# An encoder of dilated and neighbourhood attention on one core: bias loads spread, one gate through ScalarE, splits and per-head norms moved to GpSimd, bias lines as fp32r matmuls

## The chip, the cores and the metric

The kernel runs on one core of a Trainium2 chip. Times are device microseconds of one execution of the whole program; a program is timed by the median of several runs. The engines are TensorE (PE in the profile, its weight loads PEld), VectorE (DVE), ScalarE (ACT), GpSimd (POOL) and SyncE (SP), which here issues most of the DMA transfers. Each engine takes its instructions in the order in which they stand in its own stream, and waits on semaphores for what other engines deliver. PSUM is the memory that matmuls write to, in banks; SBUF holds everything else on chip.

## The reference

One batch of 512 tokens, width 1024, 16 heads of 64, two layers, everything in float32. Layer A is dilated sliding-window attention with three dilation groups, layer B neighbourhood attention on an 8 x 64 grid. Each layer normalises its input, projects it, norms q and k per head, attends with a bias, multiplies by a SiLU gate, projects back and adds the residual. Cut to its core:

```python
def rms_norm(x, g):
    y = x * lax.rsqrt(jnp.mean(x * x, axis=-1, keepdims=True) + RMS_EPS)
    return y * g

def mixer_a(hn, w_in, w_out, q_gain, k_gain, t5_bias):
    proj = hn @ w_in                       # q, k, v of 3 groups x 16 heads, and the gate
    for g, (window, dilation) in enumerate(((128, 1), (512, 4), (2048, 16))):
        q = rms_norm(qkv[:, :, g, 0], q_gain[g])      # per head, over 64 values
        k = rms_norm(qkv[:, :, g, 1], k_gain[g])
        o, lse = dilated_group_attention(q, k, qkv[:, :, g, 2], t5_bias[g], dilation, reach)
    alpha = softmax(stack(lses), axis=0)
    return (sum(alpha * stack(outs)) * silu(gate)) @ w_out

def reference(x, ...):
    x = x + mixer_a(rms_norm(x, norm_gain[0]), ...)
    x = x + mixer_b(rms_norm(x, norm_gain[1]), ...)   # 2-D window, relative bias, same gate
    return x
```

## The kernel before

**Float32 from three matmuls.** TensorE's fp32r format is less exact than float32, so each operand is split: a high part rounded to fp32r (`h`) and a low part, the value less its high part (`l`). A product is then three fp32r matmuls, high by high, high by low and low by high (`mm3`). Weights are split on the way: a raw tile of 128 x 1024 (`wraw`, eight slots) is loaded by a DMA; ACT casts 512 columns of it to the high part (`wh`, six buffers, function `cast`, line 160), then POOL or DVE subtracts to make the low part (`wl`, five buffers, `rest`, line 167). Such a half tile is called a job here and numbered in the order in which TensorE uses it; there are 344. `splits` (line 298) runs ahead of TensorE by the depth of these buffers, and `pool[0]` (line 302) says which jobs' subtraction goes to POOL: none of the first sixteen jobs behind those of the first projection, then every second in the rest of layer A's input projections, then two in five.

**Layer A** works on head pairs `hc` = 0 to 7. For each pair there are q and k of the three groups, v, and the gate. From pair 1 on, the q and k projections are done with fewer products by sums of quarter matrices ("mixed" jobs; `b11`, `t2` and the like in `Plan.mixed` are raw tiles of it): some weight tiles are added up on the way, by POOL's own accumulating DMAs (`Plan.add`) and by DVE. While TensorE projects pair `hc + 1`, the attention of pair `hc` goes on beside it.

**The order.** TensorE's order is made by hand: `run` (line 1173) interleaves a main generator (the projections) with a side generator (the attention), on a clock that counts the estimated time of the matmuls issued so far. A generator yields times to wait by that clock; `later_on(delay, job)` (line 350) issues a piece of work when the clock has gone on by `delay` nanoseconds. The other engines' instructions are given through `Ordered.call` (line 86, so nearly everything but matmuls bears line 86 in the profile) and stand, once `held[0]` is set (from pair 0's k projection on), in the order in which the program gives them.

**The per-head norms.** The sum of squares of each head, `ss`, is an ACT square and a DVE reduction (`squares`). `head_norm` (line 439) then makes `rs`, the inverse root, by `rsqrt` (line 139): two DVE operations for a first guess (`nv` is the mean with epsilon) and three Newton steps of three operations, eleven in all on a 128 x 32 tile (q) or 128 x 16 (k), since there are eight or four heads for each of four token blocks. Four scalings by `rs` follow on DVE (`rawq` or `rawk`), and DVE takes its turn of weight subtractions between them. Their gains are folded in `gk` (line 505), which ACT applies to k.

**The biases.** `bias_lines` (line 578) makes layer A's bias once: three matmuls in plain float32 of a bucket table (`t5`, 32 x 48) with a one-hot matrix (`oh`, 32 x 896) into the bank `pl`; DVE subtracts that from a mask (`mk`), and SP writes the lines to DRAM (`l0_d`, `l12_d`). For each pair `bias_a` (line 894) loads the six tiles that its attention subtracts from its logits (`log`): two of 128 x 256 into `e0` and four of 128 x 224 into `e12`, each partition with its own shift of a line. For pairs from 2 on the call (line 1145) stands after the projection of v of the pair before; SP then issues all six one after the other. SP also issues the weight tiles, the class reordering of v (`pt`) and the store of each pair's result (`y_d`).

**The gates.** In layer B, `main_g` (line 1305) projects a pair's gate into a PSUM bank `acc`; DVE multiplies it by the row scale into `gt`, which frees the bank, and ACT takes the tanh. The three minima, exponentials (`p`, with `mn` the row's minimum and sum) and transposes of the attention (`tr`) share DVE and ACT with it.

Of the kernel before, what the change touches and what calls it, by code (L numbers as in the profile page):

```python
# [49 lines left out]
def tile_hybrid_encoder(  # L50
# [14 lines left out]
    cp = ctx.enter_context(tc.tile_pool(name="cp", bufs=1))  # L65
    big = ctx.enter_context(tc.tile_pool(name="big", bufs=1))
    wp = ctx.enter_context(tc.tile_pool(name="wp", bufs=3))
    wk = ctx.enter_context(tc.tile_pool(name="wk", bufs=2))
# [4 lines left out]
    held = [False]  # L73
# [24 lines left out]
    vec, act, pol, syn = (Ordered(e) for e in (nc.vector, nc.scalar, nc.gpsimd, nc.sync))  # L98
# [21 lines left out]
    make_identity(nc, ident)  # L120
    ones = wp.tile([P, S], F32R, tag="wh", name="ones", bufs=6)
    vec.memset(ones.bitcast(F32), 1.0)
    one = cp.tile([P, 1], F32, name="one")
    vec.memset(one, 1.0)

    xm_d = dr.tile([P, KT, S], F32, name="xm_d")
# [9 lines left out]
    mix_h = big.tile([P, 4, 4, H], F32R, tag="yh", name="mix_h")  # L136
    mix_l = big.tile([P, 4, 4, H], F32R, tag="yl", name="mix_l")

    def rsqrt(eng, r, ss, n, scale):
        v = wk.tile([P, 32], F32, tag="nv", name="nv", bufs=1)  # L140
        a = wk.tile([P, 32], F32, tag="na", name="na")
        eng.tensor_scalar(v[:, :n], ss, scale, EPS, op0=ALU.mult, op1=ALU.add)
        eng.tensor_scalar(
            r.bitcast(I32), v[:, :n].bitcast(I32), -0.5, float(0x5F3759DF), op0=ALU.mult, op1=ALU.add
        )
        for _ in range(3):
            eng.tensor_mul(a[:, :n], r, r)
            if eng is vec:
                eng.scalar_tensor_tensor(a[:, :n], a[:, :n], -0.5, v[:, :n], op0=ALU.mult, op1=ALU.mult)
                eng.scalar_tensor_tensor(r, a[:, :n], 1.5, r, op0=ALU.add, op1=ALU.mult)  # L150
                continue
            eng.tensor_mul(a[:, :n], a[:, :n], v[:, :n])
            eng.tensor_scalar(a[:, :n], a[:, :n], -0.5, 1.5, op0=ALU.mult, op1=ALU.add)
            eng.tensor_mul(r, r, a[:, :n])

    turn, pool = [0], [[2, 5]]
# [103 lines left out]
    mixed_jobs = len(plan.jobs)  # L260
# [24 lines left out]
    def load(raw):  # L285
        home(raw)
        if raw.off is None:
            return
        dst, src = raw.tile[:, : raw.cols], w[:, raw.off : raw.off + raw.cols]
        if not begun:  # L290
            syn.dma_start(dst[:, :512], src[:, :512])
            begun.append(load_x(1, 2))
            dst, src = dst[:, 512:], src[:, 512:]
        syn.dma_start(dst, src)
        if behind:
            behind.pop()()

    def splits():
        casts, queue, due = [], [], plan.loads(lead)
        for at, (raw, c, step, n) in enumerate(plan.jobs):  # L300
            first = at - start_jobs
            pool[0] = [0, 1] if first < 16 else [1, 2] if at < mixed_jobs else [2, 5]
            for r in due.get(at, ()):
                load(r)
            for add in plan.sums.get(at, ()):
                add()
            casts.append((cast(raw.tile[:, c : c + step], step), n))
            if len(casts) > 1:
                done, m = casts.pop(0)
                queue.append((*rest(*done), m))  # L310
            if len(queue) > 4:
                yield queue.pop(0)
        done, m = casts.pop(0)
        queue.append((*rest(*done), m))
        yield from queue
# [10 lines left out]
    def matmul(o, l, r, share=1, **kw):  # L326

        cols = max(r.free_size() / 2.4, l.free_size() / 1.2)
        clock[0] += (cols if r.dtype == F32R else r.free_size() * 4 / 2.4 * l.free_size() / P) / share
        nc.tensor.matmul(o, l, r, **kw)  # L330
# [19 lines left out]
    def later_on(delay, job):  # L350

        timers.append((clock[0] + delay, job))
        timers.sort(key=lambda t: t[0])
# [82 lines left out]
    def squares_soon(*args):  # L436
        later_on(800, partial(squares, *args)) if held[0] else squares(*args)

    def head_norm(raw, ss, ns):


        rs = wk.tile([P, 32], F32, tag="rs", name="rs")
        rsqrt(vec, rs[:, : 4 * ns], ss[:, : 4 * ns], 4 * ns, 1.0 / DH)

        def scale(i):
            by = rs[:, i * ns : (i + 1) * ns].unsqueeze(2).to_broadcast([P, ns, 64])
            v = raw[:, i, : ns * 64].rearrange("p (a b) -> p a b", b=64)
            return vec.tensor_mul(v, v, by)

        for i in range(4):  # L450
            later_on(600 + 1000 * i, partial(scale, i)) if held[0] else scale(i)
# [52 lines left out]
    hg = xn[:, 2 * KT : G]  # L504
    gk = cp.tile([P, 4], F32, name="gk")
    for i, (a, b) in enumerate(((0, 3), (1, 4), (2, 5), (6, 7))):
        vec.scalar_tensor_tensor(
            gk[:, i : i + 1], hg[:, a : a + 1], -SCALE, hg[:, b : b + 1], op0=ALU.mult, op1=ALU.mult
        )

    def norm(layer, k, xk):
# [66 lines left out]
    def bias_lines():  # L578

        oh = wk.tile([32, 896], F32, tag="k12", name="oh", bufs=1)  # L580
        tc.keep_in_program_order(syn.dma_start(oh, onehot))
        t5 = wk.tile([32, 48], F32, tag="e0", name="t5", bufs=1)
        syn.dma_start(t5, t5t)
        mk = wk.tile([16, 896], F32, tag="q12", name="mk", bufs=1)
        syn.dma_start(mk, maskc)
        yield 3000
        for g, (o, n) in enumerate(((0, 384), (384, 256), (640, 256))):
            pl = bank("pl")
            matmul(pl[0:16, :n], t5[:, 16 * g : 16 * g + 16], oh[:, o : o + n], start=True, stop=True)
            vec.tensor_sub(mk[:, o : o + n], mk[:, o : o + n], pl[0:16, :n])  # L590
        for j in range(4):
            syn.dma_start(l0_d[:, j, j : j + 384], mk[:, 0:384])
        syn.dma_start(l12_d, mk[:, 384:896])
        yield
# [16 lines left out]
    st = {}  # L611
# [39 lines left out]
    def normed(raw, ss, ns, key, hc):  # L651

        def go():
            with in_order() if hc == 0 else nullcontext():
                head_norm(raw, ss, ns)
            st[key, hc] = raw
            stamp[key, hc] = clock[0]

        if (key, hc) == ("rawk", 0):
            later_on(4000, go)  # L660
        elif held[0]:
            later_on(2200, go)
        else:
            go()
# [226 lines left out]
            pol.tensor_sub(l, src, h.bitcast(F32))  # L891
        stamp["ya", hc, "y"] = 0

    def bias_a(hc):
        e0 = wk.tile([P, 2, 256], F32, tag="e0", name="e0", bufs=1)
        e12 = wk.tile([P, 4, 224], F32, tag="e12", name="e12", bufs=1)
        for hd in range(2):
            h = 2 * hc + hd
            syn.dma_start(
                e0[:, hd, :],  # L900
                bass.AP(l0_d.tensor, l0_d.offset + h * 1600 + 127, [[400, 4], [-4, 32], [1, 256]]),
            )
            for g in range(2):
                syn.dma_start(
                    e12[:, 2 * hd + g, :],
                    bass.AP(l12_d.tensor, l12_d.offset + h * 512 + 256 * g + 31, [[0, 4], [-1, 32], [1, 224]]),
                )
        return e0, e12

    def bias_b(hc):  # L910
# [47 lines left out]
    def attn_a(hc):  # L958
        e0, e12 = st.pop(("e", hc))
# [182 lines left out]
        yield from v_a(hc)  # L1142
        yield "wait", ("pt", hc), 2500 if hc else 0
        if hc:
            st["e", hc + 1] = bias_a(hc + 1)
        if hc:
            yield "wait", ("border", hc + 1), 0
        yield "wait", ("gate", hc), 4000
# [120 lines left out]
    def main_qk(n):  # L1269

        raw, ss = part(n), sums()

        def evac(i, acc):
            act.activation(raw[:, i, :], acc, AF.Copy, scale=rs_n[:, i : i + 1])
            squares(raw[:, i, :], ss, i, 8)

        guard = ("qk", 2 * n - 3) if n else ("rs", "b")
        yield from project(tile_of(hn_h), tile_of(hn_l), 512, evac, guard)
        rs = wk.tile([P, 32], F32, tag="rs", name="rs")
        rsqrt(vec, rs, ss, 32, 1.0 / DH)  # L1280

        def scale(hc):
            h = 4 * (hc % 2)
            by = rs.rearrange("p (i h) -> p i h", i=4)[:, :, h : h + 4].unsqueeze(3).to_broadcast([P, 4, 4, 64])
            v = raw[:, :, 64 * h : 64 * h + 256]
            u = v.rearrange("p i (h c) -> p i h c", c=64)
            vec.tensor_mul(u, u, by)
            return v

        for hc in (2 * n, 2 * n + 1):  # L1290
            st["raw", hc] = partial(scale, hc)
            stamp["raw", hc] = clock[0]
# [12 lines left out]
    def main_g(hc):  # L1305
        acc = []
        yield from project_t(acc)
        yield ("yb", hc - 3, "y") if hc else ("rs", "all")
        third = dict(tag="e0", bufs=1) if hc % 3 == 2 else dict(tag="gt", bufs=2)
        gt = wk.tile([P, S], F32, name="gt", **third)  # L1310
        eg = wk.tile([P, S], F32, tag="eg", name="eg", bufs=1)
        tc.keep_in_program_order(vec.tensor_mul(gt, acc[0], st["rs_half"]))
        act.activation(eg, gt, AF.Tanh)
        gated(hc, gt, eg, "gate_b")

# [286 lines left out]
```

## Time and profile before

| | us |
|---|---|
| median of 3 runs | 836.58 |
| the runs | 836.58, 831.44, 837.23 |
| the profiled execution | 832.24 |
| its span on the core (first to last instruction) | 830.4 |
| TensorE busy | 817.5 |
| VectorE busy | 619.4 |
| ScalarE busy | 511.5 |
| GpSimd busy | 271.9 |

Between the span and the profiled execution's own time lie 1.84 us of start and end. TensorE's mean granted clock in it is 0.998 of full speed. The page has this slicing of the span into 40 stretches of 20.8 us; a digit is the busy share in tenths:

```profile
PE   9999999999999999999999999999999999999998
DVE  7898896897897797787786777647656758686553
ACT  8666756855855846846855837654567476766340
POOL 0073343453452542543542515321111221122220
```

Layer A fills the first two thirds, layer B the rest. How to read on: TensorE is the engine to look at, so the stretches in which it stands still are what a change can win; a busy share of another engine, averaged over the span, says little about the few places where TensorE waits for it.

### The profile page before, as it was taken

The page shows a single profiled execution, that of the slowest core. Times are in us where ns is not written, and L with a number is a line of the kernel's source. Part 1 is how long each engine was busy: PE and PEld are TensorE (multiplying, and loading weights), DVE is VectorE, ACT ScalarE, POOL GpSimd, SP SyncE. Part 2 cuts the span into 40 slices and gives each one's busy share as a digit, 9 for nine tenths or more (in the row PEclk, how much of TensorE's full clock was granted, in tenths as well). Part 3 has the DMA queues.
Part 4 walks back from the last instruction along what each step waited for, and adds up shares of the span by engine and source line. Part 5 has one row for each costly group of instructions (what it writes and reads, how often), then busy time and mean ns, then how long its engine had stood idle before and what let it go on. Part 6 is the DMA issues. An engine that isn't in the chain of part 4 may idle for free.

```text
span 830.4 us, 17546 instructions
## 1 busy us (share of the span) xinstructions
PE 817.5 (98%) x6418; PEld 660.8 (80%) x6418; DVE 619.4 (75%) x1568; ACT 511.5 (62%) x1056; POOL 271.9 (33%) x214
## 2 busy tenths in 40 slices
PE   9999999999999999999999999999999999999998
PEld 7877878888887887888887887788888787788776
DVE  7898896897897797787786777647656758686553
ACT  8666756855855846846855837654567476766340
POOL 0073343453452542543542515321111221122220
PEclk9999999999999999999999999999999999999999
DMA  9327665676676766785775664284255574635122
GB/s 349 141 62 187 173 162 142 123 174 209 118 185 205 163 162 183 161 184 168 160 158 182 146 183 166 92 309 142 93 164 134 156 205 132 192 100 151 36 102 101
DMA packets 54725, 131.92 MB, mean 159 GB/s; under 512 B 6768, under 2 KB 24112, under 8 KB 54512
## 3 DMA queue, kind: packets, MB, share of 16 engines
q1 hardware_dynamic: 48304, 108.40, 42.0%
q0 software_dynamic: 6048, 22.02, 15.1%
q8 instruction: 50, 0.82, 0.4%
q10 hardware_dynamic: 288, 0.39, 0.2%
q14 instruction: 35, 0.29, 0.1%
HBM read 111.73 MB, written 11.72 MB: 149 GB/s over the span
## 4 chain that ended last, share of the span: by engine, by line
PE 81%; DVE 7%; ACT 4%; DMA 4%; issue 2%; ACTq 0%; SPq 0%; DVEq 0%
PE acc L330 68%; PE log L330 5%; PE o L330 5%; PE tp L334 3%; DMA wraw<-in_w 3%; DVE wl L86 2%; ACT p L86 1%; ACT wh L86 1%; DMA yr<-y_d 1%; DVE rawq L86 1%; DVE na L86 1%; DVE p L86 1%; DVE ss L86 1%; DVE rs L86 1%; DVE rawk L86 0%
## 5 line engine op out<-in xcount | busy, mean ns | idle before, releaser
L86 POOL TENSOR_TENSOR wl<-wraw,wh 128x512 fp32r<-128x512 f32 (+1 forms) x146 | 200.3, 1373 | 432.0 <-PE acc L330 179.4
L86 ACT CAST wh<-wraw 128x512 fp32r<-128x512 f32 (+1 forms) x344 | 206.3, 612 | 162.1 <-PE acc L330 116.7
L86 DVE TENSOR_TENSOR wl<-wraw,wh 128x512 fp32r<-128x512 f32 (+1 forms) x198 | 150.3, 761 | 42.0 <-PE acc L330 28.6
L330 PE MATMUL acc<-wh,hn_h 128*128 128x512 f32 x424 | 172.4, 408 | 2.0 <-DVE gt L86 1.6
L330 PE MATMUL acc<-wl,hn_h 128*128 128x512 f32 x424 | 165.4, 391 | 2.6 <-DVE wl L86 2.6
L330 PE MATMUL acc<-wh,hn_l 128*128 128x512 f32 x424 | 165.4, 391 | 0.0
L86 ACT ACTIVATE p<-p,mn 128x256 f32<-128x256 f32 (+2 forms) x248 | 138.0, 583 | 34.2 <-DVE mn L86 34.0
L330 PEld LDWEIGHTS acc<-wh,hn_h 128*128 128x128 f32 x424 | 79.6, 188 | 22.0 <-issue 3.8
L330 PEld LDWEIGHTS acc<-wl,hn_h 128*128 128x128 f32 x424 | 79.9, 189 | 17.7 <-DVE wl L86 3.3
L330 PEld LDWEIGHTS acc<-wh,hn_l 128*128 128x128 f32 x424 | 79.7, 188 | 17.5
L330 PE MATMUL acc<-wh,mix_h 128*128 128x512 f32 x224 | 89.0, 397 | 0.0
L330 PE MATMUL acc<-wl,mix_h 128*128 128x512 f32 x224 | 87.4, 390 | 0.0
L330 PE MATMUL acc<-wh,mix_l 128*128 128x512 f32 x224 | 87.4, 390 | 0.0
L330 PE MATMUL acc<-hn_h,wh 128*128 128x512 f32 x192 | 78.5, 409 | 0.0
L330 PE MATMUL acc<-hn_h,wl 128*128 128x512 f32 x192 | 75.1, 391 | 0.0
L330 PE MATMUL acc<-hn_l,wh 128*128 128x512 f32 x192 | 75.0, 391 | 0.0
L86 DVE STREAM_TRANSPOSE pt<-p 128x512 f32<-128x512 f32 (+1 forms) x60 | 40.6, 687 | 23.4 <-ACT p L86 23.2
L86 DVE TENSOR_REDUCE ss<-sq 128x8 f32<-128x512 f32 (+1 forms) x80 | 43.6, 571 | 16.2 <-ACT sq L86 16.2
L330 PE MATMUL acc<-y_h,wh 128*128 128x512 f32 x128 | 51.6, 403 | 0.0
L330 PE MATMUL acc<-y_h,wl 128*128 128x512 f32 x128 | 50.0, 391 | 0.0
L330 PE MATMUL acc<-y_l,wh 128*128 128x512 f32 x128 | 49.9, 390 | 0.0
L330 PEld LDWEIGHTS acc<-wh,mix_h 128*128 128x128 f32 x224 | 42.1, 188 | 9.8 <-issue 1.6
(144 smaller groups left out, 1345.3 us busy)
## 6 DMA issues: line engine op xcount, KB each, us to landing
wraw<-in_w SPq DMA_DIRECT2D x119, 512.0 KB
wraw<-in_w POOLq DMA_DIRECT2D x42, 512.0 KB, 7.4
pt<-pt SPq DMA_DIRECT2D x106, 64.0 KB
td<-tr SPq DMA_DIRECT2D x24, 224.0 KB
pt<-td SPq DMA_DIRECT2D x24, 224.0 KB
e<-l_d SPq DMA_DIRECT2D x32, 112.0 KB
wraw<-in_w SPq DMA_DIRECT2D x6, 384.0 KB
e<-l_d SPq DMA_DIRECT2D x16, 128.0 KB
```

The source lines that it names most:

```text
L86: m = f(*args, **kw)
L330: nc.tensor.matmul(o, l, r, **kw)
L334: nc.tensor.transpose(o, i, ident)
```

## The change

Five edits:

1. **Bias loads.** `bias_a` lists its loads, the two `e0` tiles first, then the four `e12` tiles. For the pairs from 2 on (`spread=True`) only the first two are issued at once; the other four go out by timers, 7.4 to 11.0 us of estimated TensorE time later, so that other transfers of SP's stream get between them.
2. **One gate.** In layer B's pair 3, ACT copies the gate's bank to `gt`, and DVE multiplies from there.
3. **Splits.** The subtraction of low parts goes to POOL for every second job behind the first nine, not behind the first sixteen: three more (jobs 25, 27 and 29).
4. **Bias lines.** The one-hot matrix is cast to fp32r (exact for zeros and ones), the bucket table is split in a high and a low part, and each float32 matmul becomes two fp32r ones.
5. **Norms.** For the fourteen q and k norms of pairs 1 to 7 in layer A, the eleven DVE operations become two on POOL: an add of epsilon and a power of -0.5. The factor 1/64 of the mean moves into epsilon (times 64) and into `gk` (times 64), in all q and k norms.

```diff
-    one = cp.tile([P, 1], F32, name="one")
+    fixed = cp.tile([P, 2], F32, name="one")
+    one, mhalf = fixed[:, 0:1], fixed[:, 1:2]
+    vec.memset(mhalf, -0.5)
...
-            pool[0] = [0, 1] if first < 16 else [1, 2] if at < mixed_jobs else [2, 5]
+            pool[0] = [0, 1] if first < 9 else [1, 2] if at < mixed_jobs else [2, 5]
...
-    def head_norm(raw, ss, ns):
+    def head_norm(raw, ss, ns, first):
         rs = wk.tile([P, 32], F32, tag="rs", name="rs")
-        rsqrt(vec, rs[:, : 4 * ns], ss[:, : 4 * ns], 4 * ns, 1.0 / DH)
+        if held[0] and not first:
+            v = wk.tile([P, 32], F32, tag="nv", name="nv", bufs=1)[:, : 4 * ns]
+            pol.tensor_scalar(v, ss[:, : 4 * ns], DH * EPS, None, op0=ALU.add)
+            pol.tensor_tensor(rs[:, : 4 * ns], v, mhalf.to_broadcast([P, 4 * ns]), op=ALU.pow)
+        else:
+            rsqrt(vec, rs[:, : 4 * ns], ss[:, : 4 * ns], 4 * ns, 1.0, DH * EPS)
...
-            gk[:, i : i + 1], hg[:, a : a + 1], -SCALE, hg[:, b : b + 1], op0=ALU.mult, op1=ALU.mult
+            gk[:, i : i + 1], hg[:, a : a + 1], -SCALE * DH, hg[:, b : b + 1], op0=ALU.mult, op1=ALU.mult
...
-        yield 3000
+        yield 1500
+        ohr = wk.tile([32, 896], F32R, tag="e12", name="ohr", bufs=1)
+        act.copy(ohr, oh)
+        t5r = wk.tile([32, 2, 48], F32R, tag="sq", name="t5r")
+        act.copy(t5r[:, 0], t5)
+        vec.tensor_sub(t5r[:, 1], t5, t5r[:, 0].bitcast(F32))
+        yield 1500
         for g, (o, n) in enumerate(((0, 384), (384, 256), (640, 256))):
             pl = bank("pl")
-            matmul(pl[0:16, :n], t5[:, 16 * g : 16 * g + 16], oh[:, o : o + n], start=True, stop=True)
+            for i in range(2):
+                matmul(
+                    pl[0:16, :n], t5r[:, i, 16 * g : 16 * g + 16], ohr[:, o : o + n], start=i == 0, stop=i == 1
+                )
...
-    def bias_a(hc):
+    def bias_a(hc, spread=False):
...
+        def load(dst, src):
+            tc.keep_in_program_order(syn.dma_start(dst, src))
+
+        for n, args in enumerate(loads):
+            if spread and n > 1:
+                later_on(5000 + 1200 * n, partial(load, *args))
+            else:
+                syn.dma_start(*args)
...
-            st["e", hc + 1] = bias_a(hc + 1)
+            st["e", hc + 1] = bias_a(hc + 1, True)
...
-        tc.keep_in_program_order(vec.tensor_mul(gt, acc[0], st["rs_half"]))
+        src = acc[0]
+        if hc == 3:
+            act.copy(gt, src)
+            src = gt
+        tc.keep_in_program_order(vec.tensor_mul(gt, src, st["rs_half"]))
```

Three places in the engines' streams, where a row is operation, output <- inputs, and the output's shape with a count of like rows in a row.

POOL, from the end of the first projection's norm to pair 1's norms. Before:

```order
L86 TENSOR_TENSOR hn_l<-pt,hn_h 128x512
L86 DMA wraw<-in_w 128x1024 x2
L86 TENSOR_TENSOR wl<-wraw,wh 128x512
L86 DMA wraw<-in_w 128x1024 x2
L86 TENSOR_TENSOR wl<-wraw,wh 128x512
L86 DMA wraw<-in_w 128x1024
L86 TENSOR_TENSOR wl<-wraw,wh 128x512 x8
L86 DMA wraw<-in_w 128x1024
```

After (`one` is the tile that also holds the constant -0.5):

```order
L86 TENSOR_TENSOR hn_l<-pt,hn_h 128x512
L86 DMA wraw<-in_w 128x1024
L86 TENSOR_TENSOR wl<-wraw,wh 128x512 x3
L86 DMA wraw<-in_w 128x1024
L86 TENSOR_TENSOR wl<-wraw,wh 128x512
L86 DMA wraw<-in_w 128x1024 x2
L86 TENSOR_TENSOR wl<-wraw,wh 128x512
L86 DMA wraw<-in_w 128x1024
L86 TENSOR_TENSOR wl<-wraw,wh 128x512 x6
L86 TENSOR_SCALAR nv<-ss 128x32
L86 TENSOR_TENSOR rs<-nv,one 128x32
L86 TENSOR_TENSOR wl<-wraw,wh 128x512 x2
```

Three subtractions come in, ahead of an accumulating load that stood before them; and the norm of pair 1's q stands ahead of the last two of the eight subtractions (jobs 47 and 49).

SP, where pair 6's bias loads (`e`, the smaller ones the `e12` tiles) follow the reordering of pair 5's v (`pt`). Before:

```order
L86 DMA pt_5180<-pt 32x512 x8
L86 DMA wraw<-in_w 128x1024
L86 DMA e_5281<-l_d 128x1x256
L86 DMA e_5282<-l_d 128x1x224 x2
L86 DMA e_5281<-l_d 128x1x256
L86 DMA e_5282<-l_d 128x1x224 x2
L86 DMA wraw<-in_w 128x1024 x3
L86 DMA y_d<-gt 128x512
```

After:

```order
L86 DMA pt_5089<-pt 32x512 x8
L86 DMA wraw<-in_w 128x1024
L86 DMA e_5190<-l_d 128x1x256 x2
L86 DMA wraw<-in_w 128x1024 x2
L86 DMA e_5191<-l_d 128x1x224 x4
L86 DMA wraw<-in_w 128x1024
L86 DMA y_d<-gt 128x512
```

Two of the three weight tiles stand ahead of the four smaller bias loads, one behind them.

ACT, where layer B's pair 3 has its gate projected: `p,mn<-p,mn` is an exponential with its row sum, `p<-p,mn` the scaling after it. Before:

```order
L86 ACTIVATE p<-p,mn 128x256 x4
L86 CAST wh<-wraw 128x512
L86 ACTIVATE p,mn<-p,mn 128x256
L86 ACTIVATE p,mn<-p,mn 128x128
L86 ACTIVATE p,mn<-p,mn 128x256
```

After:

```order
L86 ACTIVATE p<-p,mn 128x256 x4
L86 CAST wh<-wraw 128x512
L86 COPY gt<-acc 128x512
L86 ACTIVATE p,mn<-p,mn 128x256
L86 ACTIVATE p,mn<-p,mn 128x128
L86 ACTIVATE p,mn<-p,mn 128x256
```

The copy stands ahead of four exponentials; nothing else moves there.

More of the change, by code (lines that the diff above doesn't have):

```diff
@@ L137, in tile_hybrid_encoder, with rsqrt @@
     mix_l = big.tile([P, 4, 4, H], F32R, tag="yl", name="mix_l")
-    def rsqrt(eng, r, ss, n, scale):
+    def rsqrt(eng, r, ss, n, scale, eps=EPS):
         v = wk.tile([P, 32], F32, tag="nv", name="nv", bufs=1)
         a = wk.tile([P, 32], F32, tag="na", name="na")
-        eng.tensor_scalar(v[:, :n], ss, scale, EPS, op0=ALU.mult, op1=ALU.add)
+        eng.tensor_scalar(v[:, :n], ss, scale, eps, op0=ALU.mult, op1=ALU.add)
         eng.tensor_scalar(
@@ L654, in go @@
             with in_order() if hc == 0 else nullcontext():
-                head_norm(raw, ss, ns)
+                head_norm(raw, ss, ns, hc == 0)
             st[key, hc] = raw
@@ L892, in y_split @@
         stamp["ya", hc, "y"] = 0
-    def bias_a(hc):
+    def bias_a(hc, spread=False):
         e0 = wk.tile([P, 2, 256], F32, tag="e0", name="e0", bufs=1)
         e12 = wk.tile([P, 4, 224], F32, tag="e12", name="e12", bufs=1)
+        loads = []
         for hd in range(2):
             h = 2 * hc + hd
-            syn.dma_start(
+            loads.append((
                 e0[:, hd, :],
                 bass.AP(l0_d.tensor, l0_d.offset + h * 1600 + 127, [[400, 4], [-4, 32], [1, 256]]),
-            )
+            ))
+        for hd in range(2):
+            h = 2 * hc + hd
             for g in range(2):
-                syn.dma_start(
+                loads.append((
                     e12[:, 2 * hd + g, :],
                     bass.AP(l12_d.tensor, l12_d.offset + h * 512 + 256 * g + 31, [[0, 4], [-1, 32], [1, 224]]),
-                )
+                ))
+        def load(dst, src):
[5 more added lines that the diff above has]
+                syn.dma_start(*args)
         return e0, e12
@@ L1279, in main_qk @@
         rs = wk.tile([P, 32], F32, tag="rs", name="rs")
-        rsqrt(vec, rs, ss, 32, 1.0 / DH)
+        rsqrt(vec, rs, ss, 32, 1.0, DH * EPS)
         def scale(hc):
```

## The prediction

> **What bounds the kernel now.** First the page's busy times, then TensorE's waits. (Times are microseconds; a timeline row gives start, duration, engine, line, operation, out<-in, and in brackets the idle time ahead with what ended it.)
>
> ```profile
> PE 817.5 (98%) x6418; PEld 660.8 (80%) x6418; DVE 619.4 (75%) x1568; ACT 511.5 (62%) x1056; POOL 271.9 (33%) x214
> ```
>
> TensorE (PE) is busy 98% of the span and no other engine over 75%. A faster VectorE (DVE) is worth nothing by itself; what counts is each place where PE stands still. Its waits by cause (total, times, longest):
>
> ```profile
> PE acc L330 <- DVE wl L86: 2.6, 2, 1.9
> PE log L330 <- ACT k L86: 2.2, 5, 0.7
> PE acc L330 <- DVE gt L86: 1.6, 1, 1.6
> ```
>
> These three are 6.4 us of waits, so an edit can win little more than the wait it touches, or PE work that it removes. I go by the edits in that order of the program.
>
> **Bias lines in single passes.** The chain has the six passes of three float32 matmuls:
>
> ```profile
> 42.28 1.61 PE pl L330 x6
> ```
>
> Now each is two fp32r matmuls over the same columns, 2 x (384 + 256 + 256) = 1792. A 512-column fp32r matmul advances PE by 0.23 (68.52 to 68.75 below), so 1792 columns take 0.80: **-0.8**. The two casts, on ScalarE (ACT) and the subtraction on DVE are at nothing: ACT is at 62%, and PE shows no wait on either engine there; without that cover they would cost a cast each, at most 2 x 0.65 by the row at 59.15 below.
>
> **GpSimd splits sooner.**
>
> ```profile
> 68.52 0.40 PE L330 MATMUL acc<-wh,hn_l 128*128 128x512 f32 x1
> 68.75 0.40 PE L330 MATMUL acc<-wh,hn_h 128*128 128x512 f32 x1
> 69.75 0.50 PE L330 MATMUL acc<-wl,hn_h 128*128 128x512 f32 x1 [0.60 <-DVE wl L86]
> 59.15 0.65 ACT L86 CAST wh<-wraw 128x512 fp32r<-128x512 f32 x1
> 69.02 0.68 DVE L86 TENSOR_TENSOR wl<-wraw,wh 128x512 fp32r<-128x512 f32 x1
> 75.02 2.23 POOL L86 TENSOR_TENSOR wl<-wraw,wh 128x512 fp32r<-128x512 f32 x1 [13.20 <-ACT wh L86]
> ```
>
> At 68.75 PE needs 1.00 to its next matmul instead of 0.23, since job 25's low part wl comes from a busy DVE at 69.70. Its high part was there at 59.80, and GpSimd (POOL) sat idle from 61.8 to 75.02. The job is one of three that move to POOL, so wl is ready before 65: **-0.8**. One accumulating load that POOL issued ahead of that idle time now stands behind the three subtractions, at the latest at 75:
>
> ```profile
> wraw<-in_w POOLq DMA_DIRECT2D x42, 512.0 KB, 7.4
> 89.10 0.61 ACT L86 CAST wh<-wraw 128x512 fp32r<-128x512 f32 x1
> ```
>
> By the median of 7.4 to landing it is there near 83, and the first cast that reads it starts at 89.10: nothing lost while those 6 us hold.
>
> **The norms as a power on POOL.** Of fourteen norms, the first (head pair 1, q) stands where PE waits:
>
> ```profile
> 105.55 1.40 POOL L86 TENSOR_TENSOR wl<-wraw,wh 128x512 fp32r<-128x512 f32 x1 [2.29 <-ACT wh L86]
> 106.33 1.24 DVE L86 TENSOR_REDUCE ss<-sq 128x8 f32<-128x512 f32 x2
> 109.03 1.30 POOL L86 TENSOR_TENSOR wl<-wraw,wh 128x512 fp32r<-128x512 f32 x1 [2.08 <-ACT wh L86]
> 109.12 0.39 PE L330 MATMUL acc<-wl,hn_h 128*128 128x512 f32 x1
> 109.17 1.20 DVE L86 SCALAR_TENSOR_TENSOR rs<-na,rs 128x32 f32<-128x32 f32 x1
> 110.61 0.48 PE L330 MATMUL acc<-wh,hn_h 128*128 128x512 f32 x1
> 110.86 0.19 DVE L86 SCALAR_TENSOR_TENSOR rs<-na,rs 128x32 f32<-128x32 f32 x1
> 111.09 1.29 DVE L86 TENSOR_TENSOR rawq<-rawq,rs 128x512 f32<-128x512 f32 x2
> 112.30 0.68 DVE L86 TENSOR_TENSOR wl<-wraw,wh 128x512 fp32r<-128x512 f32 x1
> 113.04 0.50 PE L330 MATMUL acc<-wl,hn_h 128*128 128x512 f32 x1 [1.95 <-DVE wl L86]
> 100.00:120.00 20.00, 18.05 (x140) 13.92 (x139) 18.57 (x41) 13.57 (x26) 8.43 (x8) 0.91 0.56 147
> ```
>
> Before, the sums of squares end at 107.57, the norm's last operation at 111.05, the two rawq at 112.30, and job 48's wl at 112.98. PE, which could have had it at 110.84, starts it at 113.04: 2.20 lost. In the window 100 to 120 the granted clock is 0.91 (last row, before the DMA share): some 20 x 0.09 = 1.8 us of full-speed work lost besides.
>
> After, POOL holds the add and the power in program order ahead of job 47's wl (105.55 above, so far done early) and job 49's. Call d the time from the end of the sums to rs. POOL waits until 107.57, has rs at 107.57 + d and job 47's wl 1.40 later; PE wants that at 109.12, so it stands d - 0.15, a new wait. DVE then scales twice (1.29) and does job 48's wl (0.68), while POOL does jobs 47 and 49. The row at 109.17 shows what such company does: 1.20 for an operation that took 0.19 alone, 1.0 more. With two such stretches wl is ready at 107.57 + d + 1.29 + 0.68 + 2.0 = 111.54 + d, against PE's 110.84 + d - 0.15: 0.85 more. In all d + 0.70 is lost where 2.20 was: **d - 1.5**, and the low clock stays, since a standstill of about 1.95 remains.
>
> No row has a power; POOL's nearest prices:
>
> ```profile
> 40.75 1.86 POOL L86 TENSOR_TENSOR hn_l<-pt,hn_h 128x512 fp32r<-128x512 f32 x1 [4.14 <-ACT hn_h L86]
> 48.08 7.95 POOL L86 TENSOR_TENSOR hn_l<-pt,hn_h 128x512 fp32r<-128x512 f32 x1 [0.69 <-ACT hn_h L86]
> 55.98 2.41 POOL L86 TENSOR_TENSOR mix_l<-mixed,mix_h 128x1024 fp32r<-128x1024 f32 x1
> ```
>
> 1024 elements in 2.41 and 512 in 1.30 make 2.17 ns an element and 0.19 besides, so a simple operation on 32 elements is estimated at 0.26. Floor: the power is as cheap, d = 0.5. Ceiling: it takes the longest row, d = 0.26 + 7.95 = 8.2. I take the power as dear as an ordinary subtraction with sixteen times its elements, the row at 40.75, as the nearest to it in kind: d = 0.26 + 1.86 = 2.1, so **+0.6**.
>
> The later norms, by pair 6's q:
>
> ```profile
> 422.55 1.30 POOL L86 TENSOR_TENSOR wl<-wraw,wh 128x512 fp32r<-128x512 f32 x1 [2.79 <-DVE ss L86]
> 425.28 1.32 POOL L86 TENSOR_TENSOR wl<-wraw,wh 128x512 fp32r<-128x512 f32 x1 [0.26 <-issue]
> 426.69 0.19 DVE L86 SCALAR_TENSOR_TENSOR rs<-na,rs 128x32 f32<-128x32 f32 x1
> 434.46 0.39 PE L330 MATMUL acc<-wl,hn_h 128*128 128x512 f32 x1
> ```
>
> The pair stands between these two subtractions; the second, job 211, is done at 426.60 and used at 434.46. That is a slack of 7.9. On DVE the rawq and the next wl wait for rs, before until 426.88, now until about 423.85 + 2.1 = 425.95. So at d = 2.1 these norms cost and win nothing: the DVE operations they remove lie beside a busy PE. The seven k norms have half the elements and are taken the same.
>
> **Bias loads spread.**
>
> ```profile
> 422.13 5.42 SPq L86 DMA_DIRECT2D e<-l_d  x6
> 427.72 8.48 SPq L86 DMA_DIRECT2D wraw<-in_w  x3
> 444.00 0.62 ACT L86 CAST wh<-wraw 128x512 fp32r<-128x512 f32 x1 [5.33 <-DMA wraw<-in_w]
> 447.91 0.38 PE L330 MATMUL log<-k0h,q0h 64*128 64x256 f32 x1
> 449.00 0.38 PE L330 MATMUL log<-k0h,q0h 64*128 64x256 f32 x1 [0.72 <-ACT k L86]
> ```
>
> SyncE's queue (SP) issues six bias loads, then hangs 8.48 over three weight loads; ACT stands 5.33 until the first of them lands, then comes late with k, and PE's log matmuls wait. The list gives 2.2 for five such places and leaves out that matmuls overlap: the row at 447.91 lasts 0.38, but half the columns of a 0.23 step let the next one start 0.11 behind it, 0.27 before its end. So each place loses 0.27 more, 2.2 + 1.35 = 3.5 in all. After, two bias loads come first, then two weight loads, then the other four. The weight load that ACT waits for stands third instead of seventh, two issues of 0.9 behind 422.13 instead of behind 427.72, and no longer ends last. I count four places in full and the fifth, before the last head pair, where loads of y stand too, at half: **-3.2**. The four late bias loads go out 7.4 to 11.0 us of PE work after the first, near 433 here, well ahead of the log matmuls at 447.91 whose bias they are; the third weight load, now behind them, is needed later still.
>
> **The gate on ACT.**
>
> ```profile
> 691.70 0.51 ACT L86 ACTIVATE p<-p,mn 128x256 f32<-128x256 f32 x1
> 693.78 0.39 PE L330 MATMUL acc<-wh,hn_l 128*128 128x512 f32 x1
> 696.70 0.69 DVE L86 TENSOR_TENSOR gt<-acc,rs_half 128x512 f32<-128x512 f32 x1
> 697.44 0.50 PE L330 MATMUL acc<-wh,hn_h 128*128 128x512 f32 x1 [1.59 <-DVE gt L86]
> ```
>
> PE needs the PSUM bank that DVE empties at 696.70. The copy on ACT can do it once the last matmul ends, 694.17, plus some 0.6, so before PE arrives: **-1.6**. But the copy stands ahead of the exponential at 691.70, and this one and its three followers wait 3.1 us for it; two had waited for DVE anyway. DVE's reciprocals and transposes come about 1 us later. I cost that at nothing, as they serve matmuls behind a whole projection; without that cover, 1 of the 1.6 is lost.
>
> **Sum.** -0.8 - 0.8 + 0.6 - 3.2 - 1.6 = -5.8, on the profiled execution's 832.24 (span 830.4): 826.4. That execution lies 2.1 below the mean of it and the runs shown (836.58, 831.44, 837.23: 834.4), and 4.3 below their median. I forecast on that mean: **828.6**.
>
> **Rivals.**
> A. As worked out, 828.6. For it: each term has a wait of its own in the list of PE's waits.
> B. The first power costs a load of code, once. POOL's slowest row is such a first: 7.95 at 48.08, where its like took 1.86. With d = 8.2 the first norm costs 6.7 instead of 0.6, the other thirteen nothing: 832.5 on the profile's scale, 834.7 on the mean. Against: nothing shows that the power's code is not there. The Trainium skill, "GPSIMD Engine Reference", § 2.1 Instruction dispatch, says that the first call of freshly loaded code pays about 6 us, 5.95 measured; by that figure the estimate is 826.4 + 6.0 = 832.4, and the row at 48.08, 6.1 over its like, agrees with it in size.
> C. The power is dear every time: slower. The first norm costs d - 1.5, the six other q norms d - 7.9 each (the k norms not counted), against 6.4 won elsewhere; 7d = 55.3 or d = 7.9 is the point from which the kernel is slower, 9.1 that from which it is by over 1%. At d = 12 it is 28.7 longer: 863 on the mean. For it: no row has a power. Against: 12 us for 32 elements would be 170 times the 2.17 ns of a subtraction.
> D. The bias loads don't do it: the weight load hangs on its tile or on a full queue as before and lands as late. Then 3.2 of the sum fall away: 829.6, 831.8 on the mean. For it: SP's 8.48 is a wait of the weight loads themselves. Against: that wait begins right behind six bias loads.
>
> **Numbers.** Chances: A 0.60, B 0.12, C 0.10, D 0.12, others 0.06. About 1% (828.2 to 844.9 around 836.58) is what a measurement of this kernel can tell from no change. A, 5.8 below by the sum and 8.0 by 828.6 against 836.58, falls on either side of that line: 0.36 faster, 0.24 within. B and D are within; C is slower by 0.08 of its 0.10; the rest is shared, 0.04 faster and the others 0.05 slower or within. Faster 0.40, same 0.47, slower 0.13. Low end: d = 0.5, so the first norm costs 0.35, without stretch and without the low clock: 826.4 - (0.6 + 1.85 + 1.8) = 822.1, with the fifth load in full 821.8. High end: B at 832.5 on the upper runs, 5.0 above the profiled one: 837.5. A's own range is 821.8 to 831.4. For the low end a rule bears: the Trainium skill, "TensorE: Matmul & The Clock Gate", Part 1, lets the clock fall after an idle window of about 3.4 us; the 0.91 here followed an idle of 1.95, so the trace does not agree, and by the rule 1.8 would stay in the low end, 823.6.
>
> **What would show it.** POOL: two operations per norm, together about 2; over 8 sinks A. PE: no wait for wl near 69, one of 2 or so near 109 for POOL instead of DVE; no log <- k waits, ACT idle before v's cast under 1 us; no gt wait in layer B. Wrong would be a PE wait for rs, for p after the gate copy, or for a late bias.

## The result, and the profile after

| | before | changed |
|---|---|---|
| median, us | 834.01 (4 runs) | 868.61 (4 runs, 868.26 to 869.58) |
| ratio | 1 | 1.041, 95% interval 1.0377 to 1.0443 |
| profiled execution, us (span) | 832.24 (830.4) | 868.66 (866.9) |

The change makes the kernel 4.1% slower; forecast were 828.6 and at most 837.5. First the changed kernel's busy times, TensorE's waits (total, times, longest), and GpSimd's groups of the two powers (count, busy, mean ns of one, idle before):

```profile
PE 830.0 (96%) x6418; PEld 669.9 (77%) x6418; DVE 602.1 (69%) x1413; ACT 515.9 (60%) x1059; POOL 332.3 (38%) x245
```

```profile
PE tp L336 <- DVE gt L86: 17.3, 6, 4.2
PE acc L332 <- POOL wl L86: 5.5, 1, 5.5
PE acc L332 <- DVE wl L86: 4.7, 2, 3.1
PE tp L336 <- DVE k0l L86: 2.0, 2, 1.3
```

```profile
L86 POOL TENSOR_TENSOR rs<-nv,one 128x32 f32<-128x32 f32 x7 | 38.2, 5455 | 0.6
L86 POOL TENSOR_TENSOR rs<-nv,one 128x16 f32<-128x16 f32 x7 | 20.5, 2934 | 0.6
```

Two of the waits that the change aimed at are gone from TensorE's list: no `log <- ACT k`, and no `acc <- DVE gt`. New are 17.3 us of q's transposes (`tp`) that wait for VectorE, 2.0 of k's, 5.5 for a weight subtraction on GpSimd, and 3.1 near 72. The power takes 5.46 us for 32 elements and 2.93 for 16: 0.16 us an element and 0.4 besides.

Pair 1's q norm, in rows of the three engines' timelines (start, duration, engine, operation, idle time ahead in brackets) and one window (granted clock after the engines' busy times):

```profile
112.40 1.24 DVE L86 TENSOR_REDUCE ss<-sq 128x8 f32<-128x512 f32 x2
114.12 5.46 POOL L86 TENSOR_TENSOR rs<-nv,one 128x32 f32<-128x32 f32 x1
114.96 0.39 PE L332 MATMUL acc<-wh,hn_h 128*128 128x512 f32 x1
119.56 2.94 POOL L86 TENSOR_TENSOR wl<-wraw,wh 128x512 fp32r<-128x512 f32 x2
120.86 0.80 PE L332 MATMUL acc<-wl,hn_h 128*128 128x512 f32 x1 [5.52 <-POOL wl L86]
...
113.00:127.00 14.00, 8.48 (x85) 6.47 (x88) 8.03 (x9) 4.28 (x8) 10.95 (x6) 0.76 0.60 141
```

The sums end at 113.64 and rs at 119.58: the prediction's d is 5.9. Job 47's subtraction comes behind it on GpSimd, and TensorE stands 5.90 - 0.23 = 5.7, where it stood 2.2 before; the clock of 0.76 over 14 us takes another 3.4 of full-speed work (before, by the prediction, 1.8).

Pair 6's q norm, where the prediction saw 7.9 us of slack (the last row is again a window):

```profile
452.92 1.29 DVE L86 TENSOR_REDUCE ss<-sq 128x8 f32<-128x512 f32 x2
454.31 1.30 POOL L86 TENSOR_TENSOR wl<-wraw,wh 128x512 fp32r<-128x512 f32 x1 [2.79 <-PE acc L332]
456.08 5.46 POOL L86 TENSOR_TENSOR rs<-nv,one 128x32 f32<-128x32 f32 x1
461.57 0.69 DVE L86 TENSOR_TENSOR rawq<-rawq,rs 128x512 f32<-128x512 f32 x1 [7.36 <-POOL rs L86]
462.16 1.60 POOL L86 TENSOR_TENSOR wl<-wraw,wh 128x512 fp32r<-128x512 f32 x1
462.18 2.13 DVE L86 TENSOR_TENSOR wl<-wraw,wh 128x512 fp32r<-128x512 f32 x1
465.44 2.18 DVE L86 TENSOR_TENSOR rawq<-rawq,rs 128x512 f32<-128x512 f32 x1
465.47 1.59 POOL L86 TENSOR_TENSOR wl<-wraw,wh 128x512 fp32r<-128x512 f32 x1
469.35 0.86 DVE L86 TENSOR_TENSOR gt<-gt,o 128x128 f32<-128x128 f32 x4
469.68 0.55 PE L336 MATMUL tp<-ident,rawq 128*128 128x128 f32 x3 [2.84 <-DVE gt L86]
...
466.00:476.00 10.00, 7.16 (x29) 5.58 (x28) 6.60 (x12) 5.14 (x11) 5.58 (x5) 0.83 0.93 232
```

And the start and the end of the same chain in the kernel before:

```profile
421.16 1.29 DVE L86 TENSOR_REDUCE ss<-sq 128x8 f32<-128x512 f32 x2
430.52 1.17 DVE L86 TENSOR_TENSOR rawq<-rawq,rs 128x512 f32<-128x512 f32 x1
432.22 0.87 DVE L86 TENSOR_TENSOR gt<-gt,o 128x128 f32<-128x128 f32 x4
434.92 0.60 PE L334 MATMUL tp<-ident,rawq 128*128 128x128 f32 x4
```

The transposes of q need all four scalings of rawq, and start once the first gt product has been made behind them. Before, gt began 2.7 us ahead of the transposes. After, DVE stands 7.36 for rs (1.4 of it while GpSimd finishes a subtraction that stands ahead of the power), and two of its operations last 2.1 and 2.2 instead of 0.7, each beside a GpSimd subtraction that stands behind the power. gt begins 15.1 after the sums (454.21 to 469.35), before 9.8 (422.45 to 432.22): 5.4 later, against a cover of 2.7. TensorE stands 2.84 by the row, and the window's clock of 0.83 takes another 1.7 of 10 us. All six pairs from 2 on stand like this, by 1.9 to 4.2 in their rows.

Near 72 the changed kernel stands still as well:

```profile
71.70 0.40 PE L332 MATMUL acc<-wh,mix_h 128*128 128x512 f32 x1
75.22 0.79 PE L332 MATMUL acc<-wl,mix_h 128*128 128x512 f32 x1 [3.13 <-DVE wl L86]
```

By start to start, less a step of 0.23 as in the prediction, that is 3.3. This is job 26, between jobs 25 and 27, whose subtractions moved to GpSimd; its own stays on DVE.

### The profile page after: what moved, and what is told of

The parts are those of the page before. It is cut to its first block, busy times and chain, and to the rows that moved or that the text cites. A ratio compares the mean times of both kernels' runs of the same rounds, so it can differ in the third digit from the quotient of the medians.

```text
span 866.9 us, 17398 instructions
## 1 busy us (share of the span) xinstructions
PE 830.0 (96%) x6418; PEld 669.9 (77%) x6418; DVE 602.1 (69%) x1413; ACT 515.9 (60%) x1059; POOL 332.3 (38%) x245
## 4 chain that ended last, share of the span: by engine, by line
PE 75%; DVE 11%; issue 3%; POOL 3%; ACT 3%; DMA 2%; SPq 2%; DVEq 0%; POOLq 0%; ACTq 0%
PE acc L332 62%; PE log L332 5%; PE tp L336 4%; DVE wl L86 3%; PE o L332 3%; POOL rs L86 3%; DVE rawq L86 2%; SPq L86 2%; DMA e<-l_d 1%; DVE rawk L86 1%; DMA wraw<-in_w 1%; ACT p L86 1%; DVE pt L86 1%; DVE p L86 1%; DVE ss L86 1%
## 5 line engine op out<-in xcount | busy, mean ns | idle before, releaser
L86 POOL TENSOR_TENSOR wl<-wraw,wh 128x512 fp32r<-128x512 f32 (+1 forms) x149 | 205.5, 1381 | 380.1 <-PE acc L332 235.6
L86 DVE TENSOR_TENSOR wl<-wraw,wh 128x512 fp32r<-128x512 f32 (+1 forms) x195 | 159.0, 817 | 46.4 <-PE acc L332 31.0
L332 PE MATMUL acc<-hn_h,wh 128*128 128x512 f32 x192 | 81.3, 423 | 0.0
L332 PE MATMUL acc<-hn_l,wh 128*128 128x512 f32 x192 | 77.4, 403 | 0.0
L332 PE MATMUL acc<-hn_h,wl 128*128 128x512 f32 x192 | 77.3, 403 | 0.0
L86 DVE TENSOR_TENSOR rawq<-rawq,rs 128x512 f32<-128x512 f32 x32 | 32.7, 1034 | 50.1 <-POOL rs L86 50.1
L86 POOL TENSOR_TENSOR rs<-nv,one 128x32 f32<-128x32 f32 (+1 forms) x14 | 58.7, 4195 | 1.2
L332 PEld LDWEIGHTS acc<-wl,mix_h 128*128 128x128 f32 x224 | 42.6, 190 | 12.0 <-DVE wl L86 3.6
L86 ACT ACTIVATE sq<-rawk 128x256 f32<-128x256 f32 (+1 forms) x48 | 23.3, 488 | 47.9 <-DVE rawk L86 45.8
```

What stands on the lines that cost most here:

```text
L86: m = f(*args, **kw)
```

## The experiments

All ratios are to the kernel before, run beside it on the same chip, with 95% intervals; kernels of different experiments are compared by these ratios. Standstills near 70 are given start to start, less 0.23. Two theories stood at the start: that the power's latency makes the whole loss, through rs, and that the other edits cost too.

**The power away.** In the changed kernel, the norms back on DVE:

```diff
-        if held[0] and not first:
+        if False:
```

> The changed kernel with the fourteen norms back on DVE as Newton steps, the other four edits kept. Theory 1 (the power's latency is the whole loss: DVE waits for rs, and the transposes of rawq behind it make TensorE wait and lose its clock): no wait of tp for DVE near the norms, 826 to 830. Rival (the other edits cost too, as the 3.3 us standstill near 72 in the changed kernel suggests): 834 or more, with a standstill of 2 to 3 us near 70 still there.

830.14 us, 0.9961 (0.9941 to 0.998). Both were half right: the waits of tp for gt shrink from 17.3 to 0.8, those for k0l from 2.0 to none, so the power makes all of the loss and some 38 us; but a standstill of 3.28 near 71 stays, and the four other edits win 0.4% together, where the forecast had 6.4 us or 0.8%.

**The power alone**, on the kernel before (edit 5 and nothing else):

> The kernel before with the fourteen norms as a power on GpSimd and nothing else. Theory 1: everything the change loses and none of what it wins, 870 to 876. Rival (the edits hurt each other, the power alone is mild): under 860.

863.9 us, 1.0356 (1.0321 to 1.039). This lies between the two, 6 under theory 1 and 4 over the rival. The whole change is slower than this part of it, by 4.7 us or 0.54% with an interval of 0.47, so beside a power the other edits win nothing and seem to cost; which of them does was not tried.

**The q norms alone.**

```diff
-        if held[0] and not first:
+        if held[0] and not first and ns == 8:
```

> The changed kernel with the power for the seven q norms alone; k norms on DVE. Theory 1, with the q power at 5.5 us as what counts and the k power at 2.9 us within the slack: 862 to 869, the waits of tp unchanged. Rival (both matter by their length): about 848.

861.51 us, 1.0319 (1.0279 to 1.036). Just under the range, and the waits of tp for gt are 16.3, nearly as before; but the k powers, 2.93 us long, were not within the slack: they make 868.61 - 861.51 = 7.1 of the loss, the q powers the other 31.4. (By the ratios the k powers cost 0.91%, with an interval of 0.52.)

**GpSimd's detour without the power's length.** This kernel leaves out the inverse root: a product with -0.5 stands in the power's place.

```diff
-pol.tensor_tensor(rs[:, : 4 * ns], v, mhalf.to_broadcast([P, 4 * ns]), op=ALU.pow)
+pol.tensor_tensor(rs[:, : 4 * ns], v, mhalf.to_broadcast([P, 4 * ns]), op=ALU.mult)
```

> The changed kernel with a multiplication by -0.5 in place of the power, on GpSimd at the same place: the inverse root is left out, so rs is half the negative sum. Theory 1 (the length of the power): the multiplication takes 0.3 us, the waits of tp go, 826 to 832. Rival (the detour over GpSimd's queue and the company of two engines, not the power's length): 845 or more.

828.89 us, 0.9938 (0.9915 to 0.996). Theory 1 holds. GpSimd's group of that product:

```profile
L86 POOL TENSOR_TENSOR rs<-nv,one 128x32 f32<-128x32 f32 x7 | 1.7, 242 | 0.6
```

0.24 us for 32 elements is the 0.26 that the prediction had worked out for a simple operation. At that price the detour over GpSimd costs nothing, and pair 1's standstill shrinks from 2.2 to 1.0, with 0.5 for GpSimd's subtraction ahead of it. So it is the length of the power, with what it holds up, and not the move to GpSimd as such that hurts.

**The power in two halves**, so that DVE can scale the first two token blocks earlier:

```diff
-            pol.tensor_tensor(rs[:, : 4 * ns], v, mhalf.to_broadcast([P, 4 * ns]), op=ALU.pow)
+            for a in (0, 2 * ns):
+                pol.tensor_tensor(
+                    rs[:, a : a + 2 * ns], v[:, a : a + 2 * ns], mhalf.to_broadcast([P, 2 * ns]), op=ALU.pow
+                )
```

> The changed kernel with each power in two calls, the first two token blocks and then the other two, so that DVE can start scaling after the first. Theory 1 (what counts is when DVE gets rs and the four scalings behind it): the waits of tp fall from 17 us to under 6, 845 to 855. Rival (what counts is GpSimd's whole time, or DVE waits for the whole tile): 864 or more.

844.13 us, 1.0114 (1.0089 to 1.0138), just under the range; the waits of tp for gt fall from 17.3 to 4.9. GpSimd is not busy any less (336.7 us against 332.3), so its whole busy time is not what counts, and an earlier start of DVE's scalings helps, as theory 1 says.

**The other edits one by one**, all with the norms on DVE. Bias loads and gate only (the casts ahead of the bias lines go too, and are left out below):

```diff
-            pool[0] = [0, 1] if first < 9 else [1, 2] if at < mixed_jobs else [2, 5]
+            pool[0] = [0, 1] if first < 16 else [1, 2] if at < mixed_jobs else [2, 5]
...
-            for i in range(2):
-                matmul(
-                    pl[0:16, :n], t5r[:, i, 16 * g : 16 * g + 16], ohr[:, o : o + n], start=i == 0, stop=i == 1
-                )
+            matmul(pl[0:16, :n], t5[:, 16 * g : 16 * g + 16], oh[:, o : o + n], start=True, stop=True)
```

> Only the bias loads spread and the gate on ACT; all else as before the change. By the prediction's terms 3.2 + 1.6 = 4.8 less than the kernel before: about 828.6 against 833.4. Rival (the waits removed come back elsewhere): within 1.5 us of the kernel before.

824.98 us, 0.989 (0.9867 to 0.9912): 1.1% faster than the kernel before, beyond the forecast of the two terms, and the lowest median of all kernels here. Its SP queue at pair 6, where the two weight loads now stand between the bias loads:

```profile
418.94 1.20 SPq L86 DMA_DIRECT2D e<-l_d  x2
420.31 0.84 SPq L86 DMA_DIRECT2D wraw<-in_w  x2
421.19 11.03 SPq L86 DMA_DIRECT2D e<-l_d  x4
```

Two weight loads issue in 0.84, where the three hung for 8.48. The hanging has moved to the four late bias loads, which take 11.03: the timers, 3.6 us apart from first to last, fix only their place in SP's order. ACT's row of waits for weight loads, in the kernel before and then in this one:

```profile
ACT wh L86 <- DMA wraw<-in_w: 19.4, 6, 5.3
```

```profile
ACT wh L86 <- DMA wraw<-in_w: 0.7, 1, 0.7
```

Bias loads alone (that kernel, and `if hc == 3:` becomes `if False:` in `main_g`):

> Only the bias loads spread. By the prediction's term 3.2 less than the kernel before; by loads_and_gate (824.98 on the same scale as the profiled 832.24, 7.3 less) with a gate worth 1.8, about 5.5 less, 826.8. The wait 695 of acc for DVE's gt is back at 1.6 us; no log <- k waits. Rival (the gate's edit won most of it): 830 or more.

828.48 us, 0.9931 (0.991 to 0.9951): 0.69% or 5.8 us by the loads, nearer to the 5.5 than to the prediction's 3.2, and 0.41% or 3.4 for the gate, with an interval of some 1.7 on the first and 2.5 on the second. No log waits for ACT's k, and the wait for gt in layer B is back at 1.6, as expected.

Those two with the sooner splits, the bias lines as before the change:

> Bias loads spread, gate on ACT and splits sooner; norms on DVE and the bias lines as three float32 matmuls, as before the change. Theory 1 (the recast bias lines shift ACT's and DVE's work and so bring the standstill of 3.3 us near 71): no wait over 1 us near 52 or 71, 825 to 827. Rival (the sooner splits bring it): the standstill near 70 stays, 830.

829.0 us, 0.9927 (0.9904 to 0.995), and a standstill of 2.57 near 71, as the rival says. With the recast bias lines instead, and the splits as before the change:

> Bias loads spread, gate on ACT and bias lines as fp32r matmuls; norms on DVE and GpSimd's splits from the sixteenth job on, as before the change. Theory 1 (the bias lines bring the standstill): it stays, 3 us or more near 71, with job 25's wait on DVE added, 830 to 832. Rival (the sooner splits bring it): 826 to 827.

828.15 us, 0.9926 (0.9905 to 0.9948), with a standstill of 1.72 near 69 (for job 25; 0.77 in the kernel before) and a new one of 0.99 near 52. Here neither expectation is met: each of the two edits brings a standstill of its own, and each takes back some 0.36% or 3 us of what loads and gate win, with an interval of some 2.6; both together, in the first experiment, 0.7%.

**One split of the three.** Loads and gate, and only job 25's subtraction on GpSimd:

```diff
-            pool[0] = [0, 1] if first < 16 else [1, 2] if at < mixed_jobs else [2, 5]
+            pool[0] = [1, 1] if first == 10 else [0, 1] if first < 16 else [1, 2] if at < mixed_jobs else [2, 5]
```

> Loads and gate, and of the three splits only job 25's moved to GpSimd. Theory (a GpSimd subtraction stretches DVE's work beside it by about 1 us: job 25's hits the norm near 62, job 27's hits job 26's subtraction near 72): the 2.57 standstill near 71 of the kernel with all three falls to about 1.5, DVE's wl of job 26 is 0.7 long again; 825 to 826. Rival (the moved accumulating load or ACT's order causes it): 2.5 stays.

826.68 us, 0.992 (0.9893 to 0.9947), a little above the range; the standstill is 1.50, as the theory said. With all three splits, and then with one, DVE's row of job 26's subtraction:

```profile
72.08 1.76 DVE L86 TENSOR_TENSOR wl<-wraw,wh 128x512 fp32r<-128x512 f32 x1
```

```profile
72.50 0.69 DVE L86 TENSOR_TENSOR wl<-wraw,wh 128x512 fp32r<-128x512 f32 x1
```

Job 27's subtraction on GpSimd stretched it by 1.07. Job 25's own does the same to the k norm near 62, where one of DVE's steps takes 1.25, so even the single split shows no gain.

**The first power alone**, on loads and gate (`hc == 0` becomes `hc != 1 or ns == 4` in the call of `head_norm`, with the power's branch restored):

> Loads and gate, and the power on GpSimd for pair 1's q norm alone. The prediction's form d - 1.5 with d = 0.3 + 5.5 + 0.1 gives 4.4 more than loads_and_gate; the stall list of the changed kernel gives 5.7 - 2.2 = 3.5 and some 2 of low clock: 828.5 to 831. Rival (all of the change's loss sits in the later norms): under 826.5.

831.7 us, 0.9975 (0.9953 to 0.9997): 0.85% or 7.1 us over loads and gate, with an interval of 2.6; the time is 0.7 above the range. The standstill is 5.69 instead of 2.20, 3.5 more; the rest is the clock, 0.84 over the 20 us from 100 on, 3.2 of work. So the first norm is a fifth of the loss, and the rival falls.

**The power in quarters**, for pairs 2 to 7's q alone, on loads and gate (as in halves, with a step of `ns`, `hc < 2 or ns == 4` in the call):

> Loads and gate, and the power for the q norms of pairs 2 to 7, in four calls of eight elements, one for each token block; by 2.94 and 5.46 us for 16 and 32 elements a call takes 1.7, so DVE has its first scale 1.7 after the add, and the last after 6.9. Theory (only the time at which DVE's scalings end counts, and the slack of 3 us hides what is left): waits of tp under 0.5 each, 825 to 829, no gain over loads_and_gate. Rival (any power on GpSimd costs by its length): 838 or more.

842.91 us, 1.0118 (1.008 to 1.0156). The time is the rival's, and the theory failed: DVE did start early, and the waits of tp were still 11.9 us, 2.1 to 2.5 each. That length alone costs is no answer either, since the halves, no shorter on GpSimd, cost less. DVE, GpSimd and TensorE at pair 6:

```profile
431.45 1.29 DVE L86 TENSOR_REDUCE ss<-sq 128x8 f32<-128x512 f32 x2
434.60 6.48 POOL L86 TENSOR_TENSOR rs<-nv,one 128x8 f32<-128x8 f32 x4
436.31 0.69 DVE L86 TENSOR_TENSOR rawq<-rawq,rs 128x512 f32<-128x512 f32 x1 [3.58 <-POOL rs L86]
441.12 2.72 DVE L86 TENSOR_TENSOR rawq<-rawq,rs 128x512 f32<-128x512 f32 x1 [0.31 <-POOL rs L86]
441.70 1.58 POOL L86 TENSOR_TENSOR wl<-wraw,wh 128x512 fp32r<-128x512 f32 x1
443.76 3.79 DVE L86 TENSOR_TENSOR wl<-wraw,wh 128x512 fp32r<-128x512 f32 x1
444.19 2.80 POOL L86 TENSOR_TENSOR wl<-wraw,wh 128x512 fp32r<-128x512 f32 x2
447.48 0.87 DVE L86 TENSOR_TENSOR gt<-gt,o 128x128 f32<-128x128 f32 x4
447.81 1.11 PE L336 MATMUL tp<-ident,rawq 128*128 128x128 f32 x4 [2.44 <-DVE gt L86]
```

Beside the power itself DVE's scaling takes its usual 0.69. But three subtractions of GpSimd stand behind the power, and DVE's last scaling and its next subtraction, caught beside them, end about 0.6 after theirs: 2.7 and 3.8 us. The last scaling starts 8.4 after the sums, before 8.1; gt starts 14.7 after them, before 9.8. That made a refined theory: not only a late rs, but the work that the power holds up on GpSimd, when it comes beside DVE's.

**The company away.** In the changed kernel, the two GpSimd subtractions behind the q powers of pairs 2 to 6 go to DVE (in the trace those behind pair 1's and pair 7's are still on GpSimd):

```diff
-            pool[0] = [0, 1] if first < 9 else [1, 2] if at < mixed_jobs else [2, 5]
+            alone = first > 32 and (first - 1) % 32 in (3, 5)
+            pool[0] = [0, 1] if first < 9 or (alone and at < mixed_jobs) else [1, 2] if at < mixed_jobs else [2, 5]
```

> The changed kernel with the two GpSimd subtractions that follow each q power (jobs 3 and 5 of each pair) given to DVE. Theory (a late rs and, as much, GpSimd's postponed subtractions, which stretch DVE's rawq and wl behind it by 1.5 us each, make the transposes late): DVE's operations there last 0.7 again, one subtraction of 0.6 is added between them, so each wait of tp falls from 3.0 by about 2.3 to under 1; 855 or less. Rival (only the late rs counts): the waits stay at 3 or grow by 0.6, 868 to 873.

857.58 us, 1.0289 (1.0254 to 1.0324). Standstills at the q transposes of pairs 3 to 6 fall from 2.83 to 0.47 in their rows, as the theory said, though DVE has more to do; that of pair 7, whose company stays, is 1.82 as against 1.86. Pair 2's does not fall (4.47 against 4.15): there gt stands behind a scaling by the k norm's rs, for which DVE waits 3.47. The time misses the range by 2.6, and the k powers, 2.93 us long and with subtractions beside them, now make waits in their place:

```profile
PE tp L337 <- DVE k0l L86: 9.7, 5, 2.5
PE tp L337 <- DVE gt L86: 8.2, 6, 4.5
442.95 1.29 DVE L86 TENSOR_REDUCE ss<-sq 128x8 f32<-128x512 f32 x2
457.00 0.87 DVE L86 TENSOR_TENSOR gt<-gt,o 128x128 f32<-128x128 f32 x4
```

The last two rows are pair 6's. With them the three traces fit one account, in which TensorE waits for what gt comes later than the cover of 2.7: in the changed kernel it comes 5.4 later than before and the row says 2.84; in quarters, with the company but an early rs, 5.0 later and 2.44; without the company, with a late rs and one more subtraction on DVE, 3.0 later and 0.47.

## Why the prediction was wrong

*The step that failed* is the one on the later norms: "That is a slack of 7.9 ... So at d = 2.1 these norms cost and win nothing". The slack was read at TensorE's next use of GpSimd's subtraction. It was not read at the other consumer: rs goes by DVE's four scalings to the transposes, and those had 2.7 us of cover, not 7.9. Nor was it asked what the subtractions behind the power do to DVE when they come late. With the power's true price, d = 5.9, the prediction's own sum still gives no more than 826.4 + 3.8 = 830.2, so the price alone does not explain 868.6. With q in the changed kernel worth 31.4 us and the first of it 7.1, the six later q norms cost 24 us, 4 each, and the seven k norms 7.1; all of it was put down as nothing. (The split by norms is from differences of runs, with intervals of 2.6 to 4.3 us.) The prediction even wrote that DVE's rawq waits for rs, and set rs at 425.95 against 426.88 before; it did not ask what would happen if rs came later than that.

*The size of d* failed with it. The power was taken as 1.86 and is 5.46, within the bounds of 0.5 to 8.2 for d, but on the other side of the middle: the row "nearest in kind" was near in nothing but the engine. The form for the first norm was near: d + 0.70 gives a standstill of 6.6 for d = 5.9, and the trace shows 5.7. The term d - 1.5 gives 4.4; the first norm alone measured 7.1, of which 3.5 are standstill and the rest clock, which the prediction held as lost already.

*Rival C* was the one that came true, and its point from which it decides was wrong for the same reason: with d - 7.9 for each later norm it asked for d = 7.9, and the kernel is 34.6 us slower at a d of 5.9 in pair 1 and 7.3 in pair 6 (454.21 to 461.54). Its chance of 0.10 rested on an argument about 170 times an element's price; measured are 0.16 us an element, 73 times.

*Rival B* fell: the first power takes 5.46 and the second 5.45 (114.12 and, for pair 2, 185.34), so no first call is dearer. The Trainium skill's 6 us for freshly loaded code ("GPSIMD Engine Reference", § 2.1) is not seen in any of the fourteen.

*Bias loads and gate* were right in mechanism. The loads were short in size: -3.2 forecast, some -5.8 measured by ratios, with an interval of 1.7. For the gate it is -1.6 and some -3.4, with an interval of 2.5 that still holds the forecast. Rival D fell with the row of 0.84 and with ACT's waits for weight loads, 19.4 before and 0.7 after. The late bias loads went out from 421.19 on and not near 433, but no log waits for them.

*Sooner splits* failed: "-0.8" became +3. Job 25's wait did go, but GpSimd's subtractions fell beside DVE's norm and beside job 26's subtraction and stretched both, and TensorE's wait moved one job on. The prediction knew the stretch, and used it at pair 1 only.

*Bias lines* failed too: the six matmuls are shorter (0.27 us each in place of 0.37), and the edit costs 3 us. In the trace with the splits as before, DVE's first product for the mixed operand starts later than before the change (49.30 against 47.16; 1.1 of it since the two rawq ahead take 2.40 in place of 1.28, beside a GpSimd subtraction), ACT's cast of it and its rawk follow, and TensorE waits 0.8 for rawk. That the casts and the moved generator steps do this was not tried one by one; it stays argued.

*A sum in the chances* is out by 0.01: A's 0.24 with B and D within makes 0.48 for the same, not 0.47. Nothing rests on it.

## What to carry to other kernels

When an operation moves to another engine, follow its result to every consumer, and read the slack at the one with the least, not at the queue that it joins. Price an operation that no row shows by its ceiling when its place has a cover of a few microseconds, since the loss begins at the cover and not at the middle of the range. And count the work that queues up behind a long operation: it comes later in a bunch, beside work that it did not meet before.

## What the runs showed of the hardware that was not expected

A GpSimd subtraction and DVE operations beside it held each other up in these traces, and either lost. In the kernel before the row at 48.08 took 7.95, read in the prediction as a first call, while DVE's operations beside it took their usual 0.67 and 1.2. In the changed kernel the same subtraction took 1.30, and DVE's operations near it were the long ones:

```profile
47.27 2.39 DVE L86 TENSOR_TENSOR rawq<-rawq,rs 128x512 f32<-128x512 f32 x2
47.82 1.30 POOL L86 TENSOR_TENSOR hn_l<-pt,hn_h 128x512 fp32r<-128x512 f32 x1 [1.67 <-ACT hn_h L86]
51.96 2.88 POOL L86 TENSOR_TENSOR mix_l<-mixed,mix_h 128x1024 fp32r<-128x1024 f32 x1 [2.84 <-ACT mix_h L86]
52.53 3.40 DVE L86 TENSOR_TENSOR mixed<-mixed,pt 128x1024 f32<-128x1024 f32 x1
```

A power on GpSimd did not do this: DVE's 0.69 beside it, in quarters, is its time alone.

A low clock does not follow every short standstill, and no run here shows what decides. Pair 1's standstill of 2.20 is the same in the kernel with loads and gate, where the same stretch ran at full clock, not at 0.91:

```profile
100.00:120.00 20.00, 18.05 (x178) 14.30 (x183) 18.71 (x41) 13.47 (x27) 8.25 (x7) 1.00 0.58 146
```

Of 25 runs of the kernel before on one chip, the four at a mean clock of 1.0 took 830.4 to 831.8, the five at 0.995 took 833.3 to 838.3; so the scatter of this kernel goes in part with the clock. The Trainium skill ("TensorE: Matmul & The Clock Gate", Part 1) has a window of activity that runs on freely, so that the same program may meet it at another phase; these runs do not speak against that, while the fall behind an idle time of 1.95, under the window of about 3.4 that it states, does not follow from it.
